# Left-hand forms three products behind in the seven-product projections of a hybrid encoder block

## The chip, the core and the metric

The kernel runs on one core of a Trainium2 chip. The metric is the device time of one execution in microseconds; less is better. The core has five engines that run their own instruction streams: PE (TensorE, matrix products), DVE (VectorE), ACT (ScalarE), POOL (GpSimd) and SP (SyncE, which here only issues transfers). They wait for one another through semaphores.

## The reference

The input x has 2048 rows of 1024 numbers, float32. One layer is computed:

```python
h = rms_norm(x, norm1_g[l])
z = h @ w_in[l]
q, k, v, xr, yr = jnp.split(z, splits, axis=-1)
...   # attention over 8 heads; convolution and two RG-LRU scans, gated
mixed = jnp.concatenate([attn_out, lru_out], axis=-1) @ w_out[l]
x = x + mixed
h = rms_norm(x, norm2_g[l])
u = depthwise_conv(h @ w_up[l], up_conv_w[l], up_conv_b[l], 1, 1)
gate, val = jnp.split(u, 2, axis=-1)
x = x + (jax.nn.gelu(gate) * val) @ w_down[l]
...
return rms_norm(x, final_g)
```

w_up is 1024 x 6144 and w_down 3072 x 1024. The convolution runs along the rows of the sequence, with three taps for each channel.

## The kernel before, in words

**Stages.** Up to about 1210 us the kernel projects w_in, makes the scans and the attention. Then the output projection w_out runs (`emit_out`, matrix products in L1164) with the second normalisation (`scale_rows`, L1183) and the transposition of its result to `h2_d` in DRAM (`emit_h2`, L1216). From about 1420 us to the end the channel mixing runs: w_up, convolution, GeLU, w_down. The change touches the last two stages.

**Seven products.** Both projections of the channel mixing are computed by Strassen's scheme in Winograd's form: a 2 x 2 block product with seven products instead of eight. A step is one such block product: of 256 columns of w_up (128 gate and 128 value channels) with 1024 rows of the sequence, or of 256 rows with 1024 columns of w_down. There are 72 steps: 0 to 23 for one half of the sequence, 24 to 47 for the other (all w_up), 48 to 71 for w_down, eight for each of three groups of its rows. Each product is twelve matrix products (L1407): four blocks of 128 along the contraction, times three, since each operand is split into a high and a low part (`split`, L142 on ACT for the high part and L147 on DVE for the low one).

**Forms.** The split operands are called forms. The right-hand forms, 28 of them, stay for many steps and are remade in the steps 23, 47, 55 and 63 (`changes`, `remake`). The left-hand forms are made anew for each step: `a_srcs` takes the two halves of a load (`raw`), makes four sums of them on POOL (L1317, L1319, L1321, L1325) and yields seven sources; `a_forms` splits one source at each call. Sources 0 and 4 are pieces of the first half, 2 and 6 of the second, 1, 3 and 5 are sums (`s`). `raw` has three buffers (`rawp`).

**A step's order.** `step` and `down` emit the products in seven slots. After each product they advance generators by one: `before` (the tail of the step before: convolution taps in L1522, the scaled copy on ACT in L1531, GeLU, the product of gate and value in L1546), `nxt` (one left-hand form of the next step) and `side`. They also add results out of PSUM (`add`, L1488). Four PSUM banks serve seven products: product 4 goes on in bank 0's accumulation, product 5 in bank 3's, product 6 in bank 2's. Product 5 therefore waits for the addition `add(v2c, v2c, b[3])` of slot 4, which has read bank 3 before. The engines work strictly in the order of emission.

**Loads.** `load_w(i + 2)` issues the first half at the beginning of step i and the second half after slot 4 (w_up) or slot 3 (w_down), both on SP's queue.

**The side.** `sums_ahead` makes four sums of right-hand blocks for a coming remake on DVE (L1602, L1604, L1606, L1608: t3, b12, b11, b21) from loads through SP, and stores them to `t_d` or `wt_d`. Sixteen such jobs run one after another: four for the rows and five for w_down from step 2 on, the other seven from step 24 on. A job on rows takes 14 slots, a job on w_down 12.

**Pools around w_out.** `emit_out` writes its products into `ps_m` (four PSUM tiles); the second half of x's rows and the squares (`junk`) lie in `xp` and `sp_`, and the transposed pieces in a ring of four (`hs`, tag "st"). ACT stores the sum x1 to `x1_d` and then scales it in place.

Of the kernel before, what the change touches and what calls it, by code (L numbers as in the profile page):

```python
# [9 lines left out]
F32 = mybir.dt.float32  # L10
# [10 lines left out]
D = 1024  # L21
# [6 lines left out]
FT = 24  # L28
# [55 lines left out]
def block_kernel(ctx, tc, x, g1, wqkv, wxy, qkg, rope, cw, cb, wg, bg, lam, w_out, g2,  # L84
# [80 lines left out]
    with tc.manual_schedule():  # L165
# [6 lines left out]
        def opener(stack, side="left"):  # L172
            def pool(name, bufs, **kw):
                return stack.enter_context(tc.tile_pool(name=name, bufs=bufs, side=side, **kw))
            return pool
# [951 lines left out]
        mlps[0] = pool("d_ml0", 1)  # L1127
        mps[0] = pool("d_m0", 1)
        ps_m = pool("d_pm", 4, space=PSUM)
        rpool = opener(phf, "right")  # L1130
        fkp = [rpool("e_f0", 1)]
        tbp = [rpool("e_b", 1)]
# [5 lines left out]
        xp = rpool("d_x", 5)  # L1138
        hs = rpool("d_hs", 4)
        sp_ = rpool("d_s", 2)  # L1140
        ps_t = [opener(phs, "right")("d_pt", 4, space=PSUM)]
        NV = 2 * NB

# [7 lines left out]
        def emit_out(v):  # L1151
            ss = sp_.tile([128, 2], F32, tag="ss", name="ss")
            x1t[v] = []
            for r in range(2):
                n0 = 2 * v + 1 - r
                rows = slice((1 - r) * 128, (2 - r) * 128)
                ps = [ps_m.tile([128, 512], F32, tag="po", name="po") for _ in range(2)]
                x1 = xt.pop(n0)
                for i in range(2):
                    n = 0  # L1160
                    for k in (4, 5, 6, 7, 0, 1, 2, 3):
                        hi, lo = mix[v, k]
                        for lh, rh in ((hi, wo_hi), (hi, wo_lo), (lo, wo_hi)):
                            PE.matmul(ps[i], lhsT=lh[:, rows], rhs=rh[:, k, i * 512:(i + 1) * 512],  # L1164
                                      start=n == 0, stop=n == 23)
                            n += 1
                        if k % 2:
                            yield
                    cols = slice(i * 512, i * 512 + 512)
                    DVE.tensor_tensor(out=x1[:, cols], in0=ps[i], in1=x1[:, cols], op=ALU.add)  # L1170
                junk = sp_.tile([128, D], BF16, tag="junk", name="junk")
                ACT.activation(out=junk, in_=x1, func=AF.Square, accum_out=ss[:, r:r + 1])
                dma(out=x1_d[n0 // 4][n0 % 4], in_=x1, eng=ACT)
                x1t[v].append(x1)
                yield
            sums[v] = ss
            if v:
                scale_rows(v)

        def scale_rows(v):  # L1180
            y = inv_sqrt(sp_, sums.pop(v), 2, 1.0 / D, "r2")
            for r in range(2):
                ACT.activation(out=x1t[v][r], in_=x1t[v][r], func=AF.Copy, scale=y[:, r:r + 1])  # L1183

        def finish_last():

# [50 lines left out]
            return t.rearrange("p a b -> p (a b)")  # L1237

        def load_w(i):
            if i >= len(steps) or i == FT:  # L1240
                return
            raws[i] = []
            if i >= UP:
                q, rp = steps[i]
                for e in range(2):
                    raw = rawp.tile([128, KT, 128], F32, tag="raw", name="raw")
                    raws[i].append(flat(raw))
                    for k in range(4):
                        dma(out=raw.rearrange("p (r k) c -> p r k c", r=2)[:, :, k, :],
                            in_=g_d[8 * q + 4 * e + k][:, rp * 256:rp * 256 + 256].rearrange("p (r c) -> p r c", r=2))  # L1250
                    yield
                return
            for t in (steps[i][1], FT + steps[i][1]):
                raw = rawp.tile([128, KT, 128], F32, tag="raw", name="raw")
                dma(out=raw, in_=w_up[t])
                raws[i].append(flat(raw))
                yield
# [212 lines left out]
        def a_forms(i, srcs_=None):  # L1470
            if i >= len(steps):
                return
            if i == FT:
                fa[i] = fa[i - 1]
                return
            fa[i] = []
            srcs = srcs_ or a_srcs(i)
            now = next(srcs)
            while now is not None:
                then = next(srcs, None)  # L1480
                t = ap.tile([128, 2, 512], F32R, tag="a", name="fa")
                split(t[:, 0], t[:, 1], now, ACT, DVE)
                fa[i].append(cut(t))
                now = then
                yield
# [64 lines left out]

        def step(i, before, side, nxt):

            ld = load_w(i + 2)
            next(ld, None)
            b = {}
            for slot, j in enumerate((0, 1, 2, 3, 4, 5, 6)):
                own = {4: 0, 5: 3, 6: 2}.get(j, j)
# [14 lines left out]
                if slot == 6:  # L1572
                    add(g2c, u2, b[3])
                next(nxt, None)
                if slot == 4:
                    run(ld)
                next(side, None)
            run(before)

# [7 lines left out]
            for _ in range(n):  # L1587
                yield

        def sums_ahead(srcs, d, n):  # L1590

            b = []
            for m, src in enumerate(srcs):
                t = tbp[0].tile([128, 512], F32, tag=f"b{m}", name="b")
                dma(out=t, in_=src)
                b.append(t)
            yield
            for _ in range(n):
                yield
            b11, b12, b21, b22 = b  # L1600
            t3 = tbp[0].tile([128, 512], F32, tag="t3", name="t3")
            DVE.tensor_tensor(out=t3, in0=b22, in1=b12, op=ALU.subtract)  # L1602
            yield
            DVE.tensor_tensor(out=b12, in0=b12, in1=b11, op=ALU.subtract)  # L1604
            yield
            DVE.tensor_tensor(out=b11, in0=t3, in1=b11, op=ALU.add)  # L1606
            yield
            DVE.tensor_tensor(out=b21, in0=b21, in1=b11, op=ALU.subtract)  # L1608
            yield
            yield  # L1610
            for m, t in enumerate((t3, b12, b11, b21)):
                dma(out=d[:, m, :], in_=t)
            yield
            yield

        def rows_srcs(k):
# [47 lines left out]
        left = chain(wait(2), step_by_tile(0, iter(()), 3))  # L1664
        run(nxt)
        run(load_w(2))
        rows_ = (rows_srcs, lambda k: t_d[k])
        downs = [(lambda k, q=q: down_srcs(4 * q + k), lambda k, q=q: wt_d[4 * q + k]) for q in range(3)]
        sums_w = [sums_ahead(down_srcs(n), wt_d[n], 4) for n in (8, 9, 10, 11, 4, 5, 6, 7, 0, 1, 2, 3)]
        side = chain(*[sums_ahead(rows_srcs(k), t_d[k], 6) for k in range(4)], *sums_w[:5])  # L1670
        changes = {FT - 1: rows_, UP - 1: downs[2], UP + NV - 1: downs[1], UP + 2 * NV - 1: downs[0]}


# [21 lines left out]

        def down(i, before, side, nxt):

            ld = load_w(i + 2)
            next(ld, None)
            b = {}  # L1700
            x11, x12, x21, x22 = acc.pop(i)
            u = (dpool[0] if dpool else tbp[0]).tile([128, 512], F32, tag="u" if dpool else "t3", name="u2")
            for j in range(7):
# [19 lines left out]
                if j == 6:  # L1723
                    add(x12, x12, b[3])
                next(nxt, None)
                if j == 3:
                    run(ld)
                next(side, None)
            run(before)

# [35 lines left out]
        for i in range(1, len(steps)):  # L1766
# [2 lines left out]
                for _ in range(9):  # L1769
                    load_ring(*changes[i + 1])  # L1770
            what = remake(changes[i]) if i in changes else side
            nxt = chain(wait(3), a_forms(2)) if i == 1 else a_forms(i + 1)
            if i < UP:
                left = step(i, left, what if i > 1 else iter(()), nxt)
            else:
                if i == UP + 2 * NV:
                    for c in range(2):
                        t = tbp[1].tile([128, 512], F32, tag=f"b{2 + c}", name="gf_s")
                        dma(out=t, in_=gf[:, c * 512:c * 512 + 512].to_broadcast([128, 512]))
                        gf_s.append(t)  # L1780
                left = down(i, left, what, nxt)
            run(nxt)
            if i in changes:
                run(what)
            if i == FT - 1:
                side = chain(*sums_w[5:])
            if i == UP - 1:
                load_acc(UP)
            if i == UP:
# [73 lines left out]
```

## Time and profile before

| | |
|---|---|
| median of 3 runs | 2912.06 us (2911.29 to 2916.98) |
| the profiled execution | 2916.96 us |
| its span | 2915.2 us (1.8 us lie around it) |
| mean granted TensorE clock | 0.981 |
| PE busy | 2770.3 us (95%) |
| DVE busy | 2232.0 us (77%) |
| ACT busy | 1525.6 us (52%) |
| POOL busy | 713.6 us (24%) |
| DMA | 359.89 MB, 123 GB/s in the mean |

A row of the timeline begins with its start, then its length, the engine, the line, the operation, the tile written and the tile read, and how many instructions it groups. A bracket behind it is the idle time of the engine just ahead of it and what ended it. SPq and ACTq are the queues' issues on SP and ACT. In the row of a window (from:to) stand the window's length, the engine's busy time with its number of instructions, the granted clock, the DMA engines' share and GB/s.

### The profile page before, as it was taken

The numbers are of one execution on the slowest core, as the hardware profiler recorded it, in microseconds if no ns is written. First come the engines' busy times: TensorE is split into PE (matmuls) and PEld (weight loads), VectorE is DVE, ScalarE is ACT, GpSimd is POOL, SyncE is SP. The second block draws the span as 40 slices with busy tenths as digits, with TensorE's granted clock in tenths as the row PEclk, the third lists the DMA queues.
The fourth block names the chain that finished last, engine by engine and source line by source line (L and its number), as shares of the span: only waits on it lengthen the run. The fifth ranks groups of instructions, "written<-read, shape, count | busy, mean of one in ns | idle before, by whom it ended". The sixth has DMA issues, their size and how long they took to land.

```text
span 2915.2 us, 34136 instructions
## 1 busy us (share of the span) xinstructions
PE 2770.3 (95%) x12016; PEld 2191.9 (75%) x12016; DVE 2232.0 (77%) x2950; ACT 1525.6 (52%) x2312; POOL 713.6 (24%) x576
## 2 busy tenths in 40 slices
PE   8998998999999999999989999989999989999898
PEld 6666786777777777787667777867778877878787
DVE  6776676888888888656677878788787778686876
ACT  5776534777777777533543444454444453242443
POOL 5223443011111211010032232213222223222221
PEclk9999998999999999999999999999999999999999
DMA  3233243111121111467433444344432245665743
GB/s 132 92 131 121 85 156 108 44 53 44 48 53 48 50 44 48 139 232 251 151 122 109 145 146 133 108 149 158 143 116 83 87 141 177 206 199 177 235 156 119
DMA packets 234172, 359.89 MB, mean 123 GB/s; under 512 B 30928, under 2 KB 119888, under 8 KB 233872
## 3 DMA queue, kind: packets, MB, share of 16 engines
q1 hardware_dynamic: 210960, 298.98, 32.7%
q10 hardware_dynamic: 23040, 58.73, 5.3%
q8 instruction: 94, 1.54, 0.2%
q14 instruction: 78, 0.64, 0.1%
HBM read 231.34 MB, written 118.42 MB: 120 GB/s over the span
## 4 chain that ended last, share of the span: by engine, by line
PE 60%; DVE 13%; DMA 4%; issue 3%; ACT 2%; SPq 0%; DVEq 0%; ACTq 0%
PE pu L1407 35%; PE mx L815 4%; PE s L975 4%; PE s L974 4%; PE b L1013 4%; PE b L1011 4%; PE a L1001 4%; PE po L1164 3%; DVE u L1522 3%; DVE fb L147 2%; DVE fa L147 1%; DVE y L1488 1%; DMA sc<-sig_d 1%; DVE mxt L820 1%; DMA l<-lru_d 1%
## 5 line engine op out<-in xcount | busy, mean ns | idle before, releaser
L1407 PE MATMUL pu<-fb,fa 128*128 128x512 f32 x6027 | 1413.8, 396 | 65.0 <-DVE y L1488 43.9
L1407 PEld LDWEIGHTS pu<-fb,fa 128*128 128x128 f32 x6027 | 1139.4, 190 | 337.2 <-DVE y L1488 54.2
L820 DVE TENSOR_REDUCE mxt<-mx 128x2 f32<-128x1024 f32 x244 | 298.2, 1222 | 83.3 <-PE mx L815 83.0
L1317 POOL TENSOR_TENSOR s<-raw 128x512 f32<-128x512 f32 x70 | 103.1, 1472 | 1024.2 <-DMA raw<-in_w_up 569.4
L984 ACT ACTIVATE phi<-s 128x1024 fp32r<-128x1024 f32 x256 | 263.2, 1028 | 154.5 <-PE s L975 147.3
L991 DVE TENSOR_TENSOR plo<-p,phi 128x1024 fp32r<-128x1024 f32 x256 | 331.4, 1295 | 8.1 <-ACT p L985 7.9
L147 DVE TENSOR_TENSOR fa<-raw,fa 128x512 fp32r<-128x512 f32 (+1 forms) x284 | 244.2, 860 | 106.9 <-ACT fa L142 102.2
L1522 DVE SCALAR_TENSOR_TENSOR u<-y,ucw_s,u 128x1024 f32<-128x1024 f32 (+1 forms) x192 | 269.8, 1405 | 2.2 <-issue 0.4
L142 ACT ACTIVATE fa<-raw 128x512 fp32r<-128x512 f32 (+1 forms) x284 | 176.1, 620 | 181.7 <-PE pu L1407 89.5
L985 ACT ACTIVATE p<-s 128x1024 f32<-128x1024 f32 x256 | 261.3, 1021 | 0.4 <-DVE plo L991 0.3
L974 PE MATMUL s<-qa,ka 128*128 128x512 f32 x512 | 203.5, 398 | 4.0 <-ACT p L985 2.5
L975 PE MATMUL s<-qb,kb 65*128 65x512 f32 x512 | 203.8, 398 | 0.0
L147 DVE TENSOR_TENSOR fa<-s,fa 128x512 fp32r<-128x512 f32 (+1 forms) x213 | 161.0, 756 | 38.9 <-ACT fa L142 38.6
L815 PE MATMUL mx<-ka,qa 128*128 128x512 f32 x512 | 168.0, 409 | 12.0 <-DVE mxt L820 5.3
L1544 ACT ACTIVATE u<-u 128x1024 f32<-128x1024 f32 (+1 forms) x48 | 51.0, 1063 | 242.9 <-DVE u L1522 242.8
L1164 PE MATMUL po<-wo_hi,m 128*128 128x512 f32 x512 | 168.5, 405 | 4.0 <-ACT fb L1029 3.7
L1531 ACT ACTIVATE u<-y,ucb_s,ucw_s 128x1024 f32<-128x1024 f32 (+1 forms) x96 | 119.2, 1242 | 98.2 <-DVE y L1488 97.4
L815 PEld LDWEIGHTS mx<-ka,qa 128*128 128x128 f32 x512 | 139.7, 310 | 40.2 <-DVE mxt L820 9.5
L1488 DVE TENSOR_TENSOR y<-pu,u 128x512 f32<-128x512 f32 x144 | 99.2, 689 | 91.2 <-PE pu L1407 91.1
L142 ACT ACTIVATE fa<-s 128x512 fp32r<-128x512 f32 (+1 forms) x213 | 132.6, 622 | 59.9 <-PE pu L1407 32.6
L1013 PE MATMUL b<-phi,ones_r 128*65 128x512 f32 x512 | 161.2, 396 | 0.0
L1001 PE MATMUL a<-phi,vt 128*128 128x512 f32 x512 | 160.6, 395 | 0.0
(249 smaller groups left out, 4183.0 us busy)
## 6 DMA issues: line engine op xcount, KB each, us to landing
raw<-in_w_up SPq DMA_DIRECT2D x94, 512.0 KB
raw<-g_d SPq DMA_DIRECT2D x192, 128.0 KB
x_t<-x_d SPq DMA_DIRECT2D x96, 256.0 KB
x_t<-in_x SPq DMA_DIRECT2D x44, 512.0 KB
l<-lru_d SPq DMA_DIRECT2D x32, 512.0 KB
x_d<-x_t ACTq DMA_DIRECT2D x64, 256.0 KB
g_d<-u ACTq DMA_DIRECT2D x24, 512.5 KB
b<-in_w_down SPq DMA_DIRECT2D x48, 256.0 KB
```

The source lines that it names most:

```text
L142: ACT.activation(out=hi, in_=src, func=AF.Copy)
L147: e_lo.tensor_tensor(out=lo, in0=src, in1=f32(hi), op=ALU.subtract)
L815: PE.matmul(ps, lhsT=qa[u].rearrange("p (q t) -> p t q", t=4)[:, qt], rhs=ka[group(u)][:, kc * 512:(kc + 1) * 512], start=True, stop=True)
L820: DVE.tensor_reduce(out=mxt[u % 2][:, qt, 2 * kp:2 * kp + 2], in_=pair, axis=AX.X, op=ALU.max)
L974: PE.matmul(ps[:, h], lhsT=ka[g][:, keys], rhs=qa[u], start=True, stop=False)
L975: PE.matmul(ps[:, h], lhsT=kb[g][:, keys], rhs=qb[u], start=False, stop=True)
L984: ACT.activation(out=p_hi, in_=ps, func=AF.Exp)
L991: DVE.tensor_tensor(out=p_lo, in0=p, in1=f32(p_hi), op=ALU.subtract)
L1001: PE.matmul(pa[u], lhsT=vt[:, kt, group(u), 0:128], rhs=p_hi[:, h], start=kt == 0, stop=kt == 15)
L1013: PE.matmul(pb[u], lhsT=ones_r[:, 0:65], rhs=p_hi[:, h], start=False, stop=i == 7 and h == 1)
L1407: PE.matmul(ps, lhsT=lh, rhs=rh, start=start and n == 0, stop=stop and n == 2, skip_group_check=more)
L1522: DVE.scalar_tensor_tensor(out=u[:, 0:w], in0=y[:, o:o + w], scalar=ucw_s[:, t * FT + f, o:o + 1], in1=u[:, 0:w], op0=ALU.mult, op1=ALU.add)
```

## The change

The left-hand forms now come from one stream, `forms`, which runs through all steps and starts three slots behind: slots 3 to 6 of a step make forms 0 to 3 of the next step, and its own slots 0 to 2 make forms 4 to 6. The step before the second half of the sequence, which keeps its left-hand forms, gets seven empty calls. The loads come from a second stream, `loads`: at slot 1 of step i the second half of step i + 1's weights, at slot 3 the first half of step i + 2's. The jobs of `sums_ahead` all take 14 slots, two steps, at fixed places: loads in slot 0 and t3 in slot 5 of an even step; b12, b11 and b21 in slots 0, 1 and 5 of an odd one, stores in its slot 6. Six instead of five jobs on w_down run in the first part. Around w_out, `ps_m` asks for two more tiles that nothing uses, the second scaled row goes to a tile of its own (`xs`), and `junk` to the ring of `hs`.

```diff
         ps_m = pool("d_pm", 4, space=PSUM)
+        for _ in range(2):
+            ps_m.tile([128, 512], F32, tag="po", name="po")
...
+        xsp = rpool("d_xs", 1)
...
-                junk = sp_.tile([128, D], BF16, tag="junk", name="junk")
+                junk = hs.tile([128, D], BF16, tag="st", name="junk")
...
             for r in range(2):
-                ACT.activation(out=x1t[v][r], in_=x1t[v][r], func=AF.Copy, scale=y[:, r:r + 1])
+                t = x1t[v][r]
+                if r and v:
+                    t = xsp.tile([128, D], F32, tag="xs", name="xs")
+                ACT.activation(out=t, in_=x1t[v][r], func=AF.Copy, scale=y[:, r:r + 1])
+                x1t[v][r] = t
...
         def load_w(i):
-            if i >= len(steps) or i == FT:
+            if i >= len(steps):
+                return
+            if i == FT:
+                yield
+                yield
                 return
...
             if i == FT:
                 fa[i] = fa[i - 1]
+                for _ in range(7):
+                    yield
                 return
...
         def step(i, before, side, nxt):
 
-            ld = load_w(i + 2)
-            next(ld, None)
             b = {}
...
                 next(nxt, None)
-                if slot == 4:
-                    run(ld)
+                if slot in (1, 3):
+                    next(loads, None)
                 next(side, None)
...
-        def sums_ahead(srcs, d, n):
+        def sums_ahead(srcs, d):
...
-            yield
-            for _ in range(n):
+            for _ in range(5):
                 yield
             b11, b12, b21, b22 = b
             t3 = tbp[0].tile([128, 512], F32, tag="t3", name="t3")
             DVE.tensor_tensor(out=t3, in0=b22, in1=b12, op=ALU.subtract)
             yield
+            yield
             DVE.tensor_tensor(out=b12, in0=b12, in1=b11, op=ALU.subtract)
             yield
             DVE.tensor_tensor(out=b11, in0=t3, in1=b11, op=ALU.add)
-            yield
+            for _ in range(4):
+                yield
             DVE.tensor_tensor(out=b21, in0=b21, in1=b11, op=ALU.subtract)
-            yield
             yield
             for m, t in enumerate((t3, b12, b11, b21)):
                 dma(out=d[:, m, :], in_=t)
-            yield
             yield
...
         run(load_w(2))
+        loads = chain(wait(1), *(load_w(n) for n in range(3, len(steps))))
+        forms = chain(wait(3), *(a_forms(n) for n in range(2, len(steps))))
...
-        side = chain(*[sums_ahead(rows_srcs(k), t_d[k], 6) for k in range(4)], *sums_w[:5])
+        side = chain(*[sums_ahead(rows_srcs(k), t_d[k]) for k in range(4)], *sums_w[:6])
...
         def down(i, before, side, nxt):
 
-            ld = load_w(i + 2)
-            next(ld, None)
...
-                if j == 3:
-                    run(ld)
+                if j in (1, 3):
+                    next(loads, None)
...
-            nxt = chain(wait(3), a_forms(2)) if i == 1 else a_forms(i + 1)
             if i < UP:
-                left = step(i, left, what if i > 1 else iter(()), nxt)
+                left = step(i, left, what if i > 1 else iter(()), forms)
...
-                left = down(i, left, what, nxt)
-            run(nxt)
+                left = down(i, left, what, forms)
             if i in changes:
                 run(what)
             if i == FT - 1:
-                side = chain(*sums_w[5:])
+                side = chain(*sums_w[6:])
```

How the instructions move is seen at three places. The first is DVE in step 9, an odd step with sums, from the taps of the value half to the addition that frees bank 3 for product 5 (`y1<-pu,y1`; `fa` is the low part of a left-hand form, `raw` and `s` its sources, `u` and `y` the convolution's tiles, `b` and `t3` the sums of the side). Before:

```order
L1522 SCALAR_TENSOR_TENSOR u1_12723<-y1_12721,ucw_s_12725,u1_12723 128x1024 x2
L147 TENSOR_TENSOR fa_14030<-s_14004,fa_14030 128x512
L1604 TENSOR_TENSOR b_13867<-b_13867,b_13865 128x512
L1488 TENSOR_TENSOR u2_12724<-pu_14013,u2_12724 128x512
L1522 SCALAR_TENSOR_TENSOR u0_12722<-y0_12720,ucw_s_12725,u0_12722 128x1024
L147 TENSOR_TENSOR fa_14051<-raw_13949,fa_14051 128x512
L1606 TENSOR_TENSOR b_13865<-t3_14011,b_13865 128x512
L1522 SCALAR_TENSOR_TENSOR u0_12722<-y0_12720,ucw_s_12725,u0_12722 128x1024
L1488 TENSOR_TENSOR y1_12721<-pu_14034,u2_12724 128x512
L147 TENSOR_TENSOR fa_14070<-s_14003,fa_14070 128x512
L1608 TENSOR_TENSOR b_13869<-b_13869,b_13865 128x512
L1488 TENSOR_TENSOR y1_12721<-pu_14055,y1_12721 128x512
```

Now:

```order
L1615 TENSOR_TENSOR b_13862<-b_13862,b_13860 128x512
L1535 SCALAR_TENSOR_TENSOR u1_12736<-y1_12734,ucw_s_12738,u1_12736 128x1024 x2
L147 TENSOR_TENSOR fa_14025<-s_13926,fa_14025 128x512
L1617 TENSOR_TENSOR b_13860<-t3_13969,b_13860 128x512
L1501 TENSOR_TENSOR u2_12737<-pu_14009,u2_12737 128x512
L1535 SCALAR_TENSOR_TENSOR u0_12735<-y0_12733,ucw_s_12738,u0_12735 128x1024
L147 TENSOR_TENSOR fa_14048<-raw_13887,fa_14048 128x512
L1535 SCALAR_TENSOR_TENSOR u0_12735<-y0_12733,ucw_s_12738,u0_12735 128x1024
L1501 TENSOR_TENSOR y1_12734<-pu_14031,u2_12737 128x512
L147 TENSOR_TENSOR fa_14071<-raw_13932,fa_14071 128x512
L1501 TENSOR_TENSOR y1_12734<-pu_14051,y1_12734 128x512
```

Four sums stood ahead of the addition (t3 stands right ahead of the first row shown); now two do, and the others come behind it or in the step before. The number of forms ahead of it is the same; they are forms 4 to 6 of this step and form 0 of the next, and were forms 0 to 3 of the next.

The second place is SP's queue in the steps 2 to 4, around the first stores of sums (`t_d0`). Before:

```order
L90 DMA raw_13070<-in_w_up 128x1024
L90 DMA raw_13106<-in_w_up 128x1024
L90 DMA raw_13213<-in_w_up 128x1024
L90 DMA t_d0_93<-t3_13132 128x512
L90 DMA t_d0_93<-b_12988 128x512
L90 DMA t_d0_93<-b_12986 128x512
L90 DMA t_d0_93<-b_12990 128x512
L90 DMA raw_13253<-in_w_up 128x1024
L90 DMA b_13279<-h2_d0_89 128x512
```

Now:

```order
L90 DMA raw_13008<-in_w_up 128x1024
L90 DMA raw_13053<-in_w_up 128x1024
L90 DMA raw_13149<-in_w_up 128x1024
L90 DMA raw_13195<-in_w_up 128x1024
L90 DMA t_d0_93<-t3_13090 128x512
L90 DMA t_d0_93<-b_12983 128x512
L90 DMA t_d0_93<-b_12981 128x512
L90 DMA t_d0_93<-b_12985 128x512
L90 DMA b_13274<-h2_d0_89 128x512
```

Before, the second half of step 5's weights (`raw_13213`) went out in step 3 ahead of the stores, and the first half of step 6's (`raw_13253`) behind them. Now the last two loads ahead of the stores are the second half of step 4's weights (`raw_13149`, slot 1 of step 3) and the first half of step 5's (`raw_13195`, slot 3).

The third is ACT behind a round of w_out, where the two rows of x1 are scaled (`x_t` is x1, `r2y` the scale). Before:

```order
L90 DMA x1_d3_88<-x_t_10750 128x1024
L128 ACT_TABLE_LOAD
L128 ACTIVATE r2y_10926<-ss_10768,eps_s_138 128x2
L1183 ACTIVATE x_t_10748<-x_t_10748,r2y_10926 128x1024
L1183 ACTIVATE x_t_10750<-x_t_10750,r2y_10926 128x1024
```

Now:

```order
L90 DMA x1_d3_88<-x_t_10755 128x1024
L128 ACT_TABLE_LOAD
L128 ACTIVATE r2y_10931<-ss_10773,eps_s_138 128x2
L1189 ACTIVATE x_t_10753<-x_t_10753,r2y_10931 128x1024
L1189 ACTIVATE xs_10940<-x_t_10755,r2y_10931 128x1024
```

The order is the same; the last row writes a tile that the store in the first row doesn't read.

More of the change, by code (lines that the diff above doesn't have):

```diff
@@ L1666, in block_kernel @@
         run(load_w(2))
+        loads = chain(wait(1), *(load_w(n) for n in range(3, len(steps))))
+        forms = chain(wait(3), *(a_forms(n) for n in range(2, len(steps))))
         rows_ = (rows_srcs, lambda k: t_d[k])
         downs = [(lambda k, q=q: down_srcs(4 * q + k), lambda k, q=q: wt_d[4 * q + k]) for q in range(3)]
-        sums_w = [sums_ahead(down_srcs(n), wt_d[n], 4) for n in (8, 9, 10, 11, 4, 5, 6, 7, 0, 1, 2, 3)]
-        side = chain(*[sums_ahead(rows_srcs(k), t_d[k], 6) for k in range(4)], *sums_w[:5])
+        sums_w = [sums_ahead(down_srcs(n), wt_d[n]) for n in (8, 9, 10, 11, 4, 5, 6, 7, 0, 1, 2, 3)]
+        side = chain(*[sums_ahead(rows_srcs(k), t_d[k]) for k in range(4)], *sums_w[:6])
         changes = {FT - 1: rows_, UP - 1: downs[2], UP + NV - 1: downs[1], UP + 2 * NV - 1: downs[0]}
```

## The prediction

> **What bounds the kernel now.** I read the page first (its busy times, then its costliest groups), then the waits of PE, PE's timeline at its gaps, and last the timelines of DVE, POOL and SP in single steps.
>
> ```profile
> span 2915.2 us, 34136 instructions
> PE 2770.3 (95%) x12016; PEld 2191.9 (75%) x12016; DVE 2232.0 (77%) x2950; ACT 1525.6 (52%) x2312; POOL 713.6 (24%) x576
> L1407 PE MATMUL pu<-fb,fa 128*128 128x512 f32 x6027 | 1413.8, 396 | 65.0 <-DVE y L1488 43.9
> ```
>
> PE is busy for 95% of the span. The change can return only PE's idle time, and of that the projections (L1407) have 65.0 us. DVE y L1488, the addition that takes a product out of its PSUM bank, releases most of it. On which side the change falls depends on whether that addition comes earlier or later in a step.
>
> ```profile
> PE pu L1407 <- DVE y L1488: 8.8, 8, 1.7
> PE pu L1407 <- DVE y L1488: 4.8, 6, 1.3
> 1468.29 21.18 PE L1407 MATMUL pu<-fb,fa 128*128 128x512 f32 x84 [4.16 <-DVE y L1488]
> 1494.72 5.46 PE L1407 MATMUL pu<-fb,fa 128*128 128x512 f32 x12 [5.25 <-DVE y L1488]
> 1598.08 38.91 PE L1407 MATMUL pu<-fb,fa 128*128 128x512 f32 x168 [1.67 <-DVE y L1488]
> 1638.59 39.14 PE L1407 MATMUL pu<-fb,fa 128*128 128x512 f32 x168 [1.60 <-DVE y L1488]
> 2164.74 232.10 PE L1407 MATMUL pu<-fb,fa 128*128 128x512 f32 x1008 [1.31 <-DVE y L1488]
> ```
>
> The first two rows are PE's waits in 1500 to 1860 us (steps 3 to 22) and in 1950 to 2396 us (steps 25 to 46): 8.8 + 4.8 = 13.6 us, in columns of sum, times and longest. The others are PE's timeline; the bracket is the gap ahead of the row. All these gaps stand ahead of product 5 of a step, which opens bank 3 again. The last row has 1008 matmuls, twelve steps, without a gap: 232.10/12 = 19.34 us a step, 2.76 us a product. So those steps have slack.
>
> The slack is read in one of them, step 42. Its first product starts at 2164.74 + 6.286 × 19.34 = 2286.3 us (six steps and two products after product 5 of step 35); its product 5 at 2300.1 us, 13.8 us later. I call this count t.
>
> ```profile
> 2286.48 0.69 DVE L1488 TENSOR_TENSOR y<-pu,u 128x512 f32<-128x512 f32 x1 [1.47 <-PE pu L1407]
> 2289.07 1.53 DVE L147 TENSOR_TENSOR fa<-raw,fa 128x512 fp32r<-128x512 f32 x1 [1.89 <-ACT fa L142]
> 2290.53 2.60 DVE L1522 SCALAR_TENSOR_TENSOR u<-y,ucw_s,u 128x1025 f32<-128x1025 f32 x2
> 2293.04 0.68 DVE L147 TENSOR_TENSOR fa<-s,fa 128x512 fp32r<-128x512 f32 x1
> 2293.64 0.68 DVE L1488 TENSOR_TENSOR u<-pu,u 128x512 f32<-128x512 f32 x1
> 2294.24 1.28 DVE L1522 SCALAR_TENSOR_TENSOR u<-y,ucw_s,u 128x1025 f32<-128x1025 f32 x1
> 2295.43 0.68 DVE L147 TENSOR_TENSOR fa<-raw,fa 128x512 fp32r<-128x512 f32 x1
> 2296.04 1.28 DVE L1522 SCALAR_TENSOR_TENSOR u<-y,ucw_s,u 128x1025 f32<-128x1025 f32 x1
> 2297.23 0.68 DVE L1488 TENSOR_TENSOR y<-pu,u 128x512 f32<-128x512 f32 x1
> 2297.84 0.68 DVE L147 TENSOR_TENSOR fa<-s,fa 128x512 fp32r<-128x512 f32 x1
> 2298.43 0.68 DVE L1488 TENSOR_TENSOR y<-pu,y 128x512 f32<-128x512 f32 x1
> 2284.88 1.29 POOL L1317 TENSOR_TENSOR s<-raw 128x512 f32<-128x512 f32 x1 [14.05 <-DMA raw<-in_w_up]
> ```
>
> From 2289.07 on, DVE works without a pause until the decisive addition (2298.43) ends at 2299.11, t = 12.8. That leaves 1.0 us. One row is long: the form at 2289.07 takes 1.53 instead of 0.68 us. It runs beside the last of POOL's four left-hand sums, which follow one another from 2284.88 (1.29 us each, so about 5.2 us). Without that meeting the addition would end at t = 12.04, with 1.76 us of slack. POOL's block now lies where DVE mostly waits: the idle times of 1.47 and 1.89 us stand in the brackets.
>
> **The change: POOL's block moves into DVE's full stretch.** The second half of each load of left-hand weights now goes out at slot 1 of every step. Its buffer is freed by the low form that sits at t = 2.8 (the place of 2289.07), so the issue comes at about t = 3.5. How long a load takes, and what happens when the block meets DVE's work, is shown by step 2, where the block is already early:
>
> ```profile
> 1478.33 1.49 SPq L90 DMA_DIRECT2D raw<-in_w_up  x2
> 1482.34 1.49 POOL L1317 TENSOR_TENSOR s<-raw 128x512 f32<-128x512 f32 x1 [13.58 <-DMA raw<-in_w_up]
> 1483.91 2.15 POOL L1319 TENSOR_TENSOR s<-s,raw 128x512 f32<-128x512 f32 x1
> 1486.02 2.27 POOL L1321 TENSOR_TENSOR raw<-raw 128x512 f32<-128x512 f32 x1
> 1488.26 1.73 POOL L1325 TENSOR_TENSOR s<-raw,s 128x512 f32<-128x512 f32 x1
> 1482.59 4.55 DVE L1522 SCALAR_TENSOR_TENSOR u<-y,ucw_s,u 128x1024 f32<-128x1024 f32 x2
> 1487.07 1.78 DVE L147 TENSOR_TENSOR fa<-s,fa 128x512 fp32r<-128x512 f32 x1
> 1489.37 1.70 DVE L1522 SCALAR_TENSOR_TENSOR u<-y,ucw_s,u 128x1024 f32<-128x1024 f32 x1
> ```
>
> From 1478.33 to POOL's first sum are 4.0 us, so the block will start at t = 7.5. In step 2 it stretched two taps from 2.60 to 4.55 us, a form from 0.68 to 1.78 and a tap from 1.28 to 1.70: 1.95 + 1.10 + 0.42 = 3.5 us of DVE time lost, while POOL's own sums took up to 2.27 instead of 1.29. [...] The additions out of PSUM (0.68 us in both steps) lose nothing.
>
> [...]
>
> In the changed step DVE has four such instructions between t = 7.15 and its addition: tap, form, tap, form. The first tap is under way when the block starts; the other three meet a POOL sum each. At 0.93 us each (between the 0.42 and the 1.10 of step 2) the loss I is 2.8 us. Its bounds are the 0.85 us that one meeting costs in step 42 and the 3.5 us of step 2. I take 2.8, since a tap early in the block goes free. The addition then ends at 12.04 + I, and a step without sums ahead of it waits I − 1.76 = 1.04 us.
>
> **The sums ahead.** In the rhythm before, an odd step has four DVE sums of 0.6 us ahead of the decisive addition:
>
> ```profile
> 1631.25 0.68 DVE L1604 TENSOR_TENSOR b<-b 128x512 f32<-128x512 f32 x1
> ```
>
> This is one of them; it takes 0.60 us from its start to that of the next. They explain the gap of 1.60 us at 1638.59: −1.76 + 4 × 0.6 + 0.85 = 1.5. Afterwards two of the four, t3 and b21, lie behind the addition, and b12 and b11 stay ahead of it. That removes 1.2 us from each odd step. It also pushes the taps later by 0.6 us at least, so that a bit more of them meets POOL: I add 0.3 us. An odd step waits −1.76 + 1.2 + 2.8 + 0.3 = 2.54 us.
>
> The sum over the steady steps: odd steps with sums are 3 to 21 and 25 to 35, 16 in all, at 2.54 = 40.6 us; the other steps from 4 to 46, without the change of right-hand forms in 23 and 24, are 26 at 1.04 = 27.0 us. From 67.6 us go the 13.6 us of before: **+54.0 us**.
>
> **The forms three products behind.** Ahead of the decisive addition there are four forms before and four after; their count changes nothing in a steady step. At the start it does: step 1 no longer makes its last three forms at one go, so step 2 gets its own forms in time. Of the 5.25 us at 1494.72 about 1 stays. The twelve matmuls behind it ran at 5.46/12 = 0.455 us instead of 0.231, 2.7 us lost, and that would go too: at best −6.9, at worst 0 if lateness stays. I take −5.0. The 4.16 us at 1468.29 lie in step 1, ahead of the difference, and stay.
>
> **The change steps and the down steps** (47 to 71) I cost at nothing. In the change steps DVE is full everywhere, and the POOL block costs it the same wherever it lies. In the down steps DVE is busy for little more than two thirds:
>
> ```profile
> 2440.00:2550.00 110.00, 74.91 (x92) 1.00 0.59 194
> 2439.83 129.18 PE L1407 MATMUL pu<-fb,fa 128*128 128x512 f32 x561
> ```
>
> The windows row (DVE busy 74.91 of 110 us) is the cover, 35 us in 5.7 steps, 6 us a step, and PE runs 129 us there without a gap. A loss of 2.8 us in each step fits; if the cover were gone, 20 steps at 1 us would cost 20 us. Their changes may move by ±3 us in all.
>
> **The second scaled row (xs).** ACT scaled x_t in place and had to wait until its store had read it:
>
> ```profile
> 1376.79 1.15 ACT L1183 ACTIVATE x_t<-x_t,r2y 128x1024 f32<-128x1024 f32 x1 [2.35 <-DMA x_d<-x_t]
> 1323.47 0.98 PE L1216 MATMUL tp<-idn,x_t 128*128 128x128 f32 x7 [1.49 <-ACT x_t L1183]
> 1377.99 1.75 PE L1216 MATMUL tp<-idn,x_t 128*128 128x128 f32 x7 [3.17 <-ACT x_t L1183]
> ```
>
> With a tile of its own the wait goes. PE gets back 1.49 us in one round and, of 3.17, the 2.35 that ACT waited: **−3.8 us**. At other rounds PE has mix matmuls queued ahead and hides it. The new wait, junk in the ring of hs, costs ACT a little, and PE nothing that I can find.
>
> **The scores' banks.** The two extra tiles are never written or read. In the program as built, the first output tile stands in the same bank in both kernels and waits for the same release by ACT. I cost it at 0.
>
> **The sum.** +54.0 − 5.0 − 3.8 = +45.2 us, against the profiled execution's 2916.96 us (span 2915.2 and 1.8 around it): 2962.2. That execution is 4.9 us above the median of the runs, 2912.06; beside the median the forecast is **2957**.
>
> **The rivals.** All depend on I. With the terms above the difference is 16 × (I − 0.26) + 26 × (I − 1.76) − 22.4 us, where no bracket counts below zero. It is zero at about I = 1.7.
>
> A, the other side: the block misses DVE's full stretch, or costs one meeting as in step 42 (I = 0.85). Then the steps without sums run free and the odd ones wait 0.6 us: 9.4 − 22.4 = −13, **2899**; with no wait at all −22.4, 2890. For it: DVE has 1.76 us of slack and two sums fewer ahead of the addition. Against it: step 2, where the block met three instructions in the same place of the step. It decides if loads land more than 5 us later than I think, or if POOL yields.
>
> B, in between, I from 1.3 to 1.85: within 6 us of **2912**. It takes two meetings instead of three.
>
> C, the clock: gaps of 4.16 and 5.25 us are followed by slow matmuls (21.18 us for 84 instead of 19.34, and the 2.7 us above), gaps of 1.67 us are not (38.91 for 168). With I = 3.5 the odd steps wait 3.24 us and the sum is 2987; if 2 us of slow matmuls come behind each of the 16, **3019**. [...] Between 1.67 and 4.16 us the rows above leave it open.
>
> D: that the change doesn't do what it says holds for the banks alone, and is in the sum with 0.
>
> **How the numbers follow.** The forecast, waits of 0.5 to 1.7 us in each up step, has 0.57, with 2930 to 2988 as its own range. A has 0.20, B 0.09, C 0.07, and 0.07 is left for the down steps and for what I don't see. The range 2897 to 2992 leaves out half of A and all of C. About 0.2%, 5.8 us, is what a measurement can tell from no change. Faster by more than that: A and a piece of B and the rest, 0.23. Within: 0.09. Slower: 0.68.
>
> **What would show it.** Right: POOL's block starts about 7.5 us into each up step; the second pair of taps and the forms there take 1.7 to 2.3 and 1.7 us; PE waits ahead of product 5 in nearly every up step, 1 us in even and 2.5 in odd ones, also in the twelve steps that ran free; both gaps at the transposes are gone; the gap at the first output tile stays. Wrong: a block that starts after t = 12, taps of 1.28 us beside it, or up steps without gaps.

## The result, and the profile after

| | before | after |
|---|---|---|
| median, us | 2911.68 (4 runs, 2909.84 to 2916.98) | 3013.02 (4 runs, 3007.24 to 3020.05) |
| ratio | | 1.0346, 95% interval 1.032 to 1.0372 |
| span of the profiled execution, us | 2915.2 | 3011.1 |
| mean granted TensorE clock | 0.981 | 0.971 |

The change makes the kernel 3.5% slower, some 101 us. The direction was forecast, the size was not: 2957 was predicted, with a range that ended at 2992.

The page of the changed kernel (busy times, then two of its costliest groups; L1418 is L1407 of before, and L1535 is L1522):

```profile
span 3011.1 us, 34142 instructions
PE 2796.5 (93%) x12016; PEld 2207.3 (73%) x12016; DVE 2314.6 (77%) x2950; ACT 1516.4 (50%) x2312; POOL 782.2 (26%) x576
L1418 PE MATMUL pu<-fb,fa 128*128 128x512 f32 x6027 | 1444.1, 401 | 137.3 <-DVE y L1501 106.0
L1535 DVE SCALAR_TENSOR_TENSOR u<-y,ucw_s,u 128x1024 f32<-128x1024 f32 (+1 forms) x192 | 319.7, 1665 | 3.6 <-ACT u L1544 1.4
```

Three things stand there. PE's idle time in the projections went from 65.0 to 137.3 us, and the release is still the addition out of PSUM. PE's busy time for the same matmuls went from 1413.8 to 1444.1 us. And the convolution's taps on DVE, the same 192 instructions, take 319.7 us instead of 269.8.

PE's waits for that addition in the steps 3 to 19 and 25 to 46 (in columns of sum, times and longest) and some rows of its timeline:

```profile
PE pu L1418 <- DVE y L1501: 32.6, 15, 3.1
PE pu L1418 <- DVE y L1501: 44.3, 21, 3.1
1576.71 21.14 PE L1418 MATMUL pu<-fb,fa 128*128 128x512 f32 x84 [1.87 <-DVE y L1501]
1645.56 21.14 PE L1418 MATMUL pu<-fb,fa 128*128 128x512 f32 x84 [3.08 <-DVE y L1501]
1690.68 20.96 PE L1418 MATMUL pu<-fb,fa 128*128 128x512 f32 x84 [2.82 <-DVE y L1501]
1713.43 19.57 PE L1418 MATMUL pu<-fb,fa 128*128 128x512 f32 x84 [1.79 <-DVE y L1501]
1736.11 38.89 PE L1418 MATMUL pu<-fb,fa 128*128 128x512 f32 x168 [3.10 <-DVE y L1501]
2399.38 19.55 PE L1418 MATMUL pu<-fb,fa 128*128 128x512 f32 x84 [1.56 <-DVE y L1501]
```

Of the 42 steady up steps (3 to 22 and 25 to 46) 39 now have a gap ahead of product 5, typically 1.8 us in a step without sums ahead and 3.1 in an odd one, also the twelve steps that ran free before (the row at 2399.38 is one). Behind some of the gaps 84 matmuls take 21.1 us instead of 19.6: about eight of them take 0.43 us from start to start instead of 0.23.

Step 12 shows why. These are rows of SP, POOL and DVE; the step's product 5 begins at 1713.43, and was due at 1711.64:

```profile
1701.27 0.33 SPq L90 DMA_DIRECT2D raw<-in_w_up  x1
1704.69 1.29 POOL L1328 TENSOR_TENSOR s<-raw 128x512 f32<-128x512 f32 x1 [15.31 <-DMA raw<-in_w_up]
1706.06 2.15 POOL L1330 TENSOR_TENSOR s<-s,raw 128x512 f32<-128x512 f32 x1
1708.16 1.74 POOL L1332 TENSOR_TENSOR raw<-raw 128x512 f32<-128x512 f32 x1
1709.87 2.27 POOL L1336 TENSOR_TENSOR s<-raw,s 128x512 f32<-128x512 f32 x1
1703.63 0.68 DVE L147 TENSOR_TENSOR fa<-s,fa 128x512 fp32r<-128x512 f32 x1
1704.83 2.23 DVE L1535 SCALAR_TENSOR_TENSOR u<-y,ucw_s,u 128x1024 f32<-128x1024 f32 x1
1706.98 1.77 DVE L147 TENSOR_TENSOR fa<-raw,fa 128x512 fp32r<-128x512 f32 x1
1708.68 2.31 DVE L1535 SCALAR_TENSOR_TENSOR u<-y,ucw_s,u 128x1024 f32<-128x1024 f32 x1
1711.51 1.17 DVE L147 TENSOR_TENSOR fa<-raw,fa 128x512 fp32r<-128x512 f32 x1
1712.61 0.68 DVE L1501 TENSOR_TENSOR y<-pu,y 128x512 f32<-128x512 f32 x1
```

With the step's start at 1711.64 − 13.8 = 1697.8, the load goes out at t = 3.4 and POOL begins at t = 6.9. All four taps and forms from then up to the addition (1712.61) meet a POOL sum: 2.23, 1.77, 2.31 and 1.17 us, where 1.28, 0.68, 1.28 and 0.68 are their times alone. That is 3.6 us lost.

Where the 95.9 us between the two spans lie, worked out from the starts of the products in both traces:

| stage | difference, us |
|---|---|
| steady up steps: gaps, 81.6 instead of 13.7 | +67.9 |
| steady up steps: matmuls beyond their 19.3 us a step, 35.3 instead of 4.6 | +30.7 |
| steps 0 to 2 | −3.4 |
| change steps 23/24, 47/48, 55/56, 63/64 | −2.8 + 3.9 + 1.3 + 0.6 = +3.1 |
| the last seven down steps | +4.1 |
| ahead of the first projection | −6.5 |

### The profile page after: what moved, and what is told of

Same layout as the page of the kernel before. It is cut to its first block, busy times and chain, and to the rows that moved or that the text cites. A ratio compares the mean times of both kernels' runs of the same rounds, so it can differ in the third digit from the quotient of the medians.

```text
span 3011.1 us, 34142 instructions
## 1 busy us (share of the span) xinstructions
PE 2796.5 (93%) x12016; PEld 2207.3 (73%) x12016; DVE 2314.6 (77%) x2950; ACT 1516.4 (50%) x2312; POOL 782.2 (26%) x576
## 4 chain that ended last, share of the span: by engine, by line
PE 27%; DVE 19%; issue 5%; ACT 4%; DMA 2%; SPq 0%; POOL 0%; ACTq 0%; DVEq 0%; POOLq 0%
PE pu L1418 26%; DVE u L1535 8%; DVE y L1501 3%; DVE fa L147 2%; ACT u L1544 2%; DVE fb L147 1%; PE po L1167 1%; ACT fa L142 1%; DMA l<-lru_d 1%; DVE u L1501 1%; DVE b L1617 1%; DVE x_t L1766 1%; ACT fb L142 0%; DVE hb L925 0%; DVE m L147 0%
## 5 line engine op out<-in xcount | busy, mean ns | idle before, releaser
L1418 PE MATMUL pu<-fb,fa 128*128 128x512 f32 x6027 | 1444.1, 401 | 137.3 <-DVE y L1501 106.0
L1418 PEld LDWEIGHTS pu<-fb,fa 128*128 128x128 f32 x6027 | 1157.4, 193 | 421.7 <-ACT y L1504 62.5
L820 DVE TENSOR_REDUCE mxt<-mx 128x2 f32<-128x1024 f32 x244 | 298.1, 1222 | 81.6 <-PE mx L815 80.8
L147 DVE TENSOR_TENSOR fa<-raw,fa 128x512 fp32r<-128x512 f32 (+1 forms) x284 | 270.1, 951 | 108.2 <-ACT fa L142 108.2
L1535 DVE SCALAR_TENSOR_TENSOR u<-y,ucw_s,u 128x1024 f32<-128x1024 f32 (+1 forms) x192 | 319.7, 1665 | 3.6 <-ACT u L1544 1.4
L142 ACT ACTIVATE fa<-raw 128x512 fp32r<-128x512 f32 (+1 forms) x284 | 169.8, 618 | 72.7 <-DVE x_t L1766 32.9
```

Of the source, the lines that this page charges most:

```text
L142: ACT.activation(out=hi, in_=src, func=AF.Copy)
L147: e_lo.tensor_tensor(out=lo, in0=src, in1=f32(hi), op=ALU.subtract)
L820: DVE.tensor_reduce(out=mxt[u % 2][:, qt, 2 * kp:2 * kp + 2], in_=pair, axis=AX.X, op=ALU.max)
L1418: PE.matmul(ps, lhsT=lh, rhs=rh, start=start and n == 0, stop=stop and n == 2, skip_group_check=more)
L1535: DVE.scalar_tensor_tensor(out=u[:, 0:w], in0=y[:, o:o + w], scalar=ucw_s[:, t * FT + f, o:o + 1], in1=u[:, 0:w], op0=ALU.mult, op1=ALU.add)
```

## The experiments

**Four sums left out.** Theory 1 is that of the prediction: POOL's sums hold DVE ahead of the decisive addition. Theory 2 puts the loss on the new places of forms and DVE sums. The first run leaves POOL's four sums out of the changed kernel (the third is written over a piece of the second half, so form 2 is a sum as well).

```diff
-            s1, s2, s4 = (tap.tile([128, 512], F32, tag=f"s{n}", name="s") for n in (1, 2, 4))
-            eng.tensor_tensor(out=s1, in0=a21, in1=a22, op=ALU.add)
+            s1, s2, s4 = a22, a12, a11
...
-            eng.tensor_tensor(out=s2, in0=s1, in1=a11, op=ALU.subtract)
...
```

> The changed kernel without POOL's four left-hand sums in each step (their places are filled by plain halves of the weights, so the result is not the reference's). Theory 1 (POOL's sums hold DVE ahead of the addition that frees bank 3): the gaps ahead of product 5 vanish in all steady up steps, and with them the slow matmuls behind them; 82 us of gaps and 31 us of slow matmuls go, 3013 becomes about 2900 (2888 to 2908). Theory 2 (the place of the forms, or the new places of the DVE sums, delays the addition): DVE's order is unchanged, so most gaps stay, above 2960.

Measured: 2855.35 us (2 runs). One row of PE's timeline covers the steps 3 to 21 and most of 22 and 23:

```profile
1499.63 374.13 PE L1414 MATMUL pu<-fb,fa 128*128 128x512 f32 x1626
```

No gap is left; the order of forms and sums on DVE does no harm by itself. The time is below the expected range: beside the changed kernel's profile the steady up steps take 117 us less, and the steps 0 to 2 gain 11 us, those from 47 on 22, and the part ahead of the first projection 8. The run took away two things at once, though: POOL's work, and the waiting for its results.

**A block that comes later.** The raw buffers are given out as two for first halves and one for second halves, so that the load behind POOL's block waits for form 6.

```diff
-        rawp = rpool("e_raw", 3)
+        rawp = [rpool("e_raw", 2), rpool("e_raw1", 1)]
...
-                raw = rawp.tile([128, KT, 128], F32, tag="raw", name="raw")
+                raw = rawp[e].tile([128, KT, 128], F32, tag="raw", name="raw")
```

> The changed kernel with the three raw buffers given out as two for first halves and one for second halves. The load of a second half then waits for form 6 of its own step (slot 2) and not for form 4 (slot 0), and POOL's block starts about 13 us into the step, behind the decisive addition. All else stays. Theory 1: even up steps run without a gap, odd ones with at most 0.5 us; about 2900 (2893 to 2912), faster than before. Theory 2: as POOL's work and DVE's order are the same, the gaps stay, above 2960. Third way: the forms from sums now wait for POOL, and a new stall stands ahead of product 2 or 5 of the next step; 2915 to 2960.

Measured: 3007.43 us (4 runs), ratio 1.0318, interval 1.0304 to 1.0332. The third way named there came, 47 us beyond its range. Rows of POOL, ACT and DVE in step 12:

```profile
1702.41 1.29 POOL L1328 TENSOR_TENSOR s<-raw 128x512 f32<-128x512 f32 x1 [15.72 <-DMA raw<-in_w_up]
1705.10 0.63 ACT L142 ACTIVATE fa<-s 128x512 fp32r<-128x512 f32 x1 [3.90 <-POOL s L1330]
1705.77 1.11 DVE L147 TENSOR_TENSOR fa<-s,fa 128x512 fp32r<-128x512 f32 x1 [3.85 <-ACT fa L142]
```

Now the form in slot 4 has to wait for POOL's second sum: ACT stands for 3.90 us, and DVE behind it for 3.85, with what DVE does next queued behind. With the forms three slots behind, POOL's sums must be late enough for the addition and early enough for slot 4. Neither of the two places does both; whether one between them would was not tried.

**The rhythm of the sums alone, and the two streams alone,** each put into the kernel before.

```diff
-            yield
-            for _ in range(n):
+            for _ in range(5):
                 yield
...
-        side = chain(*[sums_ahead(rows_srcs(k), t_d[k], 6) for k in range(4)], *sums_w[:5])
+        side = chain(*[sums_ahead(rows_srcs(k), t_d[k]) for k in range(4)], *sums_w[:6])
...
```

> The kernel before with the new rhythm of the sums ahead alone (two steps each, t3 and b21 out of the way of the decisive addition; six jobs in the first part). Theory 1: an odd step waits -1.76 + 1.2 + 0.85 = 0.3 us instead of about 1.5; some 10 of the 13.6 us of gaps go: 2902 (2899 to 2906). Theory 3 (the new rhythm itself does harm): no faster than 2912.

```diff
-            ld = load_w(i + 2)
-            next(ld, None)
...
-                if slot == 4:
-                    run(ld)
+                if slot in (1, 3):
+                    next(loads, None)
...
-                left = step(i, left, what if i > 1 else iter(()), nxt)
+                left = step(i, left, what if i > 1 else iter(()), forms)
...
```

> The kernel before with the two streams (forms three slots behind, loads at slots 1 and 3) alone; sums, scaled row and banks as before. Theory 1: steps without sums wait 1.8 us as in the changed kernel; odd steps have four sums ahead of the addition instead of two, so they wait about 1.2 us more than the 3.1 there, 4.3 us, all followed by slow matmuls; with the 3 us of the scaled row 3035 (3022 to 3050). Theory 3 (the loss is in the new rhythm of the sums): below 2990.

Measured: the sums alone 2903.74 us (5 runs), ratio 0.9963, interval 0.9951 to 0.9976; the streams alone 3033.54 us (4 runs), ratio 1.0416, interval 1.04 to 1.0432. Both times are where theory 1 put them. PE's waits of the first in 1500 to 1870 us, and two rows of PE's timeline of the second:

```profile
PE pu L1407 <- DVE y L1488: 5.3, 8, 1.0
```

```profile
1534.46 19.57 PE L1411 MATMUL pu<-fb,fa 128*128 128x512 f32 x84 [1.71 <-DVE y L1494]
1558.31 22.09 PE L1411 MATMUL pu<-fb,fa 128*128 128x512 f32 x84 [4.27 <-DVE y L1494]
```

The sums ahead are the good half of the change and the streams the bad one. Two more sums ahead of the addition make the odd gap 4.27 instead of 3.08 us, the expected 1.2 more. That the first time fits is in part luck: some 10 of the 13.7 us of gaps in steady up steps were to go, and 5.8 went. The rest of its gain isn't in these steps.

**Sums that nothing reads.** To part DVE's longer instructions beside POOL's sums (contention, below) from the waiting for results, POOL makes its sums and the forms are split from plain halves. A second run keeps only the first two sums; a third puts all four into the kernel with the late block.

```diff
-            s1, s2, s4 = (tap.tile([128, 512], F32, tag=f"s{n}", name="s") for n in (1, 2, 4))
+            d1, d2, d4 = (tap.tile([128, 512], F32, tag=f"s{n}", name="s") for n in (1, 2, 4))
+            s1, s2, s4 = a22, a12, a11
-            eng.tensor_tensor(out=s1, in0=a21, in1=a22, op=ALU.add)
+            eng.tensor_tensor(out=d1, in0=a21, in1=a22, op=ALU.add)
...
```

> The changed kernel; POOL makes its four left-hand sums in each step as there, at the same time, but nothing reads them: the forms are split from plain halves as in the run without them (the result is not the reference's). Theory 1 (the two engines contend for SBUF): DVE loses the same time as in the changed kernel, gaps of about 1.8 and 3.1 us in the up steps, 2985 to 3013. Rival (the loss is the forms' waiting for POOL's results): as without the sums, 2855 to 2870.

> As the one before, but POOL makes only the first two of its four sums (result not the reference's). Theory 1: each sum costs DVE about 0.9 us, so I falls from 3.5 to about 1.8: even steps wait 0 to 0.3 us, odd ones about 1.4, no slow matmuls: 2855 + 16 x 1.4 + 26 x 0.2 = 2883 (2870 to 2900). Rival (only the last sum, or the block's end, matters): as with none or as with four, under 2865 or over 2950.

> The kernel with the late block (two raw buffers for first halves, one for second halves), with four sums on POOL that nothing reads (result not the reference's). There ACT stood 3.9 to 4.6 us in each step for POOL's second sum. If that wait is what kept the late block slow: the gaps go, 2857 to 2885. If contention behind the addition is (stretched products and forms at the step's end): 2940 or more.

Measured: 2884.78 us with four sums, 2866.89 with two, 2880.75 with the late block (2 runs each). The run with four sums missed theory 1's range by 100 us, the one with two by 3. The trace of the first tells why; a row of POOL in step 12, and PE's row at the product 5 after it:

```profile
1666.39 1.39 POOL L1329 TENSOR_TENSOR s<-raw 128x512 f32<-128x512 f32 x1 [12.05 <-DMA raw<-in_w_up]
1689.37 38.89 PE L1419 MATMUL pu<-fb,fa 128*128 128x512 f32 x168 [0.48 <-DVE y L1502]
```

The block starts at t = 10.6 here (step 13's product 5 was due at 1688.89, so step 12 began at 1655.8), and not at 6.9. The plain half put in the place of s4 lets form 5 read the first half of the weights too, so its buffer comes free a slot later. So the run moved the block as well, and says something else than intended: with the same work on both engines, a block 3.7 us later leaves a gap of about 0.5 us in the odd steps only. The third run settles the late block:

```profile
1499.77 383.33 PE L1419 MATMUL pu<-fb,fa 128*128 128x512 f32 x1666
```

With the late block and nothing that waits for its results, the up steps have no gap. Its slowness was the waiting of slot 4's form, not contention behind the addition.

**The same at the right time.** The plain halves are chosen so that form 4 stays the last reader of a first half. The edit is shown against the run with four sums that nothing reads; the second run again keeps only the first two sums.

```diff
-            s1, s2, s4 = a22, a12, a11
+            s1, s2, s4 = a22, a11, a22
```

> The run with four sums that nothing reads had its block not where the changed kernel has it: the plain halves put in the sums' places let form 5 read the first half too, so the next load waited for slot 1 and POOL began 11 us into the step. Here the plain halves are chosen so that form 4 is the last reader, as in the changed kernel (result not the reference's). POOL begins about 7.2 us into the step. Theory 1 (contention in DVE's full stretch): gaps of about 1.8 us in even and 3.1 us in odd up steps, with slow matmuls; 2985 to 3010. Rival (the loss is in what waits for POOL's results): 2855 to 2890, as with the block at 11 us.

> As the one before with only the first two of POOL's sums (result not the reference's). Theory 1: two meetings instead of four, so I falls from 3.5 to about 1.8: even steps wait up to 0.3 us, odd ones about 1.5 us, no slow matmuls: 2857 + 16 x 1.5 + 26 x 0.2 = 2886 (2872 to 2900). Rival: as with four, above 2950, or as with none, below 2862.

Measured: 3011.39 us with four sums (2 runs; ratio 1.0336, interval 1.0297 to 1.0375), 2900.30 with two (6 runs; ratio 0.9958, interval 0.9945 to 0.9972). The rows are POOL's first sum in step 13 and PE's waits from 1500 to 1870 us of the first, then PE's waits in the same stretch of the second:

```profile
1717.41 1.36 POOL L1329 TENSOR_TENSOR s<-raw 128x512 f32<-128x512 f32 x1 [13.92 <-DMA raw<-in_w_up]
PE pu L1419 <- DVE y L1502: 35.8, 15, 3.1
```

```profile
PE pu L1417 <- DVE y L1500: 11.1, 17, 1.0
```

With POOL back at t = 6.9 the changed kernel's time is there again, with 86 us of gaps in the steady up steps instead of 81.6, although no form waits for POOL. So POOL's sums beside DVE's instructions make the loss by themselves; that the two engines meet in SBUF, as theory 1 has it, no run shows. And it has a dose: four sums cost typically 1.8 us in an even step and 3.1 in an odd one, two cost 0.3 and 1.0, and none left no gap. Both times lie just above their expected ranges, by 1.4 and 0.3 us.

**The scaled row alone,** with `junk` in the ring of `hs`, put into the kernel before.

```diff
-                ACT.activation(out=x1t[v][r], in_=x1t[v][r], func=AF.Copy, scale=y[:, r:r + 1])
+                t = x1t[v][r]
+                if r and v:
+                    t = xsp.tile([128, D], F32, tag="xs", name="xs")
+                ACT.activation(out=t, in_=x1t[v][r], func=AF.Copy, scale=y[:, r:r + 1])
+                x1t[v][r] = t
...
```

> The kernel before with the tile of its own for the second scaled row, and junk in the ring of hs, alone. The two gaps of 1.49 and 2.35 us go: 3.8 us faster, 2908 (2906 to 2911). If another wait takes their place: 2912.

Measured: 2909.88 us (11 runs) beside 2914.25 (15 runs); ratio 0.9982, interval 0.9972 to 0.9992: 2 to 8 us, the 3.8 among them. The waits of PE on the scaled rows before, and in the changed kernel with its wait at the first output tile:

```profile
PE tp L1216 <- ACT x_t L1183: 7.4, 4, 3.2
```

```profile
PE tp L1223 <- ACT x_t L1189: 3.5, 3, 2.5
PE tp L1223 <- ACT xs L1189: 0.7, 1, 0.7
PE po L1167 <- ACT fb L1029: 3.7, 1, 3.7
```

7.4 us became 4.2, and 2.0 in the run with the row alone. The last row is the scores' banks: 3.7 us before and after, so the two extra tiles change nothing there; they were not run alone.

**A version that beats both.** The kernel before, with its forms and loads, plus the scaled row's tile and all four DVE sums behind the decisive addition.

```diff
-            yield
-            for _ in range(n):
+            for _ in range(5):
                 yield
...
             DVE.tensor_tensor(out=t3, in0=b22, in1=b12, op=ALU.subtract)
             yield
             DVE.tensor_tensor(out=b12, in0=b12, in1=b11, op=ALU.subtract)
-            yield
+            for _ in range(5):
+                yield
             DVE.tensor_tensor(out=b11, in0=t3, in1=b11, op=ALU.add)
             yield
             DVE.tensor_tensor(out=b21, in0=b21, in1=b11, op=ALU.subtract)
-            yield
             yield
...
```

> A version to beat both: the kernel before (forms and loads as there) with the tile of its own for the second scaled row, and with all four sums of the side behind the decisive addition (t3 and b12 in slots 5 and 6 of an even step, b11 and b21 in slots 4 and 5 of an odd one; two steps a job). Theory 1: no sum stands ahead of the addition, so the 13.6 us of gaps in steady up steps go; with 3 us of the scaled row 2912 - 16.6 = 2895 (2892 to 2900). If the sums delay the end of a step instead (the addition of the next step's first slot), no better than the run with the new rhythm alone, 2903.

Measured: 2885.13 us (4 runs), ratio 0.9901, interval 0.9886 to 0.9916. That is 7 us below the expected range.

```profile
1489.78 398.51 PE L1412 MATMUL pu<-fb,fa 128*128 128x512 f32 x1732
```

The steady up steps run without any gap, from 1489.78 to the change in step 23. From the first projection's product to the end the profiled execution takes 1478.6 us instead of 1497.7, so 19.1 us lie there (of some 29 by the medians, 33 between the two profiled executions): 18.2 in steady up steps, slow matmuls included. A few us are the scaled row; the rest lies ahead of the projections. The start of the first one differs between the profiled executions even for kernels with the same code up to there (1417.5 us in the kernel before, 1406.8 with the sums alone, 1410.5 with the streams alone), and I don't explain it.

## Why the prediction was right or wrong

- **The mechanism: right.** The second half's load goes out at t = 3.4 (3.5 forecast), POOL starts at 6.9 (7.5), DVE's taps take 2.2 to 2.3 us and its form 1.8, and gaps appear in the steps that were free. The run with early sums that nothing reads, with 86 us of gaps in the steady up steps, shows that POOL's sums beside DVE's instructions do it by themselves.
- **The loss I: mis-sized.** "The first tap is under way when the block starts; the other three meet a POOL sum each" put I at 2.8 us. The block came 0.6 us earlier than forecast, all four met, and step 12 lost 3.6 us. The gaps of the steady up steps sum to 81.6 us instead of 67.6 (2.85 us in the mean of the odd steps against 2.54, 1.38 in the others against 1.04): +14 us. Step 2's 3.5 us would have missed by as much on the other side, 97 us by the prediction's own terms, since in nine steps (4, 8, 14, 16 to 18, 20, 22 and 37) the block started 0.2 to 2.3 us later than in step 12 and left at most 1 us of gap. About 3.1 us in the mean fits.
- **The slack: a small slip.** The addition at t = 12.8 less the 0.85 us of one meeting is 11.95, not 12.04. This makes each forecast wait 0.1 us too long.
- **The clock: the step that failed.** The sum has nothing for slow matmuls. Rival C had 2 us of them behind each of 16 odd steps, only if I = 3.5, at 3019 us; it got a chance of 0.07 and lay outside the range. The measured 3013 lies beside it, by luck in the parts: the gaps were smaller than it assumed, and of the 16 slow stretches in the trace four lie in even steps. These matmuls cost 30.7 us more than before, three fifths of the miss of 51 us on the profiled executions (95.9 against 45.2). The prediction held that between 1.67 and 4.16 us its rows leave the matter open. But the trace of before has gaps of that size:

```profile
1945.40 19.59 PE L1407 MATMUL pu<-fb,fa 128*128 128x512 f32 x84 [2.57 <-DVE y L1488]
2588.88 145.36 PE L1407 MATMUL pu<-fb,fa 128*128 128x512 f32 x624 [2.00 <-DVE x_t L1488]
```

  Behind the first, 84 matmuls take their usual 19.6 us; behind the second, 624 take some 1.6 us more than at 2.76 us for twelve. In the trace the granted clock is 0.50 for 3.41 us behind the gap of 2.00 us, and stays at 1.00 behind the one of 2.57 us. With forecast waits of 2.54 us in 16 steps, a term for it belonged into the sum or at least into the range.
- **The sums ahead: right in size** for a stretched step: with all four sums ahead the odd gap is 4.27 us, with two 3.08, the 1.2 us forecast. Alone, in the kernel before, they bring 7 to 14 us, and 5.8 us of gaps in the steady up steps.
- **The scaled row: right.** 3.8 us forecast, 3.2 us of PE's waits gone, 2 to 8 us in time.
- **The banks: right** as far as PE's wait at the first output tile shows it, 3.7 us in both kernels.
- **Steps 1 and 2:** −5 forecast, −3.4 measured for steps 0 to 2; step 2 kept a gap of 4.05 us, since the block meets it too.
- **Change and down steps: more than forecast.** They were put at nothing, with ±3 us in all, and cost 7.2: 3.1 in the change steps, and 4.1 in the last seven down steps, which got four gaps, 3.0 us of waits, that the "cover" of 6 us a step was thought to hide. Why it fails there only was not tried.

## What to carry to other kernels

An instruction that is made earlier brings its transfers and the helper engine's work earlier too; ask what that work will run beside. Here the same four sums of POOL cost 1.8 to 3.1 us a step where DVE had no pause, and at most 0.7 us where they began 3.7 us later. A stall on PE can be priced twice, once as a wait and again as slow matmuls behind it: here 81.6 us of gaps, most of them of 1.8 to 3.1 us, came with 35.3 us of slow matmuls, and the plan was worse than the sum of its stalls. Moving small operations behind the one that others wait for (the four sums) emptied the steady up steps of gaps, 18 us, where the large change cost 101.

## What the runs showed of the hardware

- **Behind gaps of about 2 us and more on PE the granted clock was often 0.50.** In the traces of the kernels before and after, from 1495 us to the end, none of the 34 gaps from 0.3 to 1.8 us is followed within 3.5 us by a stretch at 0.50, 18 of the 27 from 1.8 to 3.5 us are, and all nine longer ones. So the length of a gap alone did not decide it. These are stretches of the changed kernel around two gaps of 3.08 us, ahead of 1509.89 and of 1862.58 (behind the stretch's length stand PE's busy time and the granted clock):

```profile
1505.94:1509.36 3.42, 0.87 (x4) 1.00 0.71 201
1509.36:1512.77 3.41, 2.88 (x7) 0.50 0.63 238
1857.51:1860.93 3.42, 1.99 (x9) 1.00 0.46 91
1860.93:1864.34 3.41, 1.76 (x8) 1.00 0.78 293
1864.34:1867.76 3.42, 3.42 (x17) 1.00 0.78 280
```

  The first gap leaves 2.55 us of the first row without a matmul, and the next row shows 0.50. The second lies with 1.43 us in one row and 1.65 in the next, and the clock stays at 1.00. At 0.50 a matmul takes 0.43 us from start to start instead of 0.23; about eight stand in 3.41 us, some 1.5 us lost.
- **DVE's instructions with both inputs in SBUF and POOL's sums got longer beside each other.** A form goes from 0.68 to 1.77 us and a tap from 1.28 to 2.31 beside POOL's sums, which go from 1.29 to 2.27; without POOL's sums the taps ran at 1.27 to 1.29 us throughout. Additions with one input in PSUM keep 0.68 us. Four sums of 1.29 us, 5.2 us in all, cost DVE some 3.5 us here.
